# Sample states read before their update, the update in the MLP, and a new start and end in a one-layer decoder step

## The chip, the cores and the metric

The kernel runs on one core of one Trainium2 chip. The metric is the device time of one execution in microseconds (us), the median of three runs. Engines are named as the profile names them: PE multiplies matrices, PEld loads its weights, DVE and ACT do elementwise work, POOL and SP here mostly issue DMAs (POOL also does a little arithmetic). SPq, POOLq and ACTq are the DMA queues of SP, POOL and ACT.

## The reference, cut to what matters

One layer of a decoder step is computed for a prompt of 256 tokens and for 8 sample tokens, each of which brings its own recurrent states. D_MODEL is 2048, all data is float32.

```
mod = silu(c) @ w_ada + b_ada                 # 2048 x 12288; sh1, sc1, gt1, sh2, sc2, gt2
h   = rmsnorm(x) * g * (1 + sc1) + sh1
z   = h @ w_in                                # 2048 x 15376
# A: spatial gating; B: HGRN2 recurrence (8 heads, dk = dv = 128)
# C: gated linear attention (4 heads, dk 128, dv 256)
S_t = diag(f_t) S_{t-1} + k_t v_t^T ;  o_t = S_t^T q_t        # B and C, per head
merged = sum_n sigmoid(z_gate[n]) * (branch[n] @ w_branch[n])
x = x + gt1 * rmsnorm(merged @ w_out) * g_post
h2 = rmsnorm(x) * g * (1 + sc2) + sh2
y2 = square(relu(h2 @ w_mlp_up)) @ w_mlp_down                 # 2048 x 8192 and back
x = x + gt2 * rmsnorm(y2) * g_post2
outputs: y_prompt, y_sample, final states of the prompt,
         updated states of the 8 samples (8 x 8 x 128 x 128 and 8 x 4 x 128 x 256), v rows
```

A sample is one token long, so its recurrence is one step: S = diag(f) S0 + k v^T and o = S^T q. The same output is also o = S0^T (f q) + (q . k) v, which needs the old state only.

## The kernel before, in words

**Products.** Activations stand transposed, with 264 columns (256 prompt tokens, 8 samples). Each float32 product is three PE products: weights and activations are both split into a high part and a low part, and PE adds hi by x-hi, hi by x-lo and lo by x-hi (lines 601, 602, 603 of `granule`). Weights come in granules of 128 x 4 x 256 (0.5 MB, the size of a buffer `raw`): `Stream.load` issues their DMAs on SP, up to LOAD_AHEAD = 5 granules ahead into 4 buffers, `Stream.split` splits them up to SPLIT_AHEAD = 2 granules ahead into 6 buffers of halves. A half is split by one ACT copy (`whi`, L109) and one DVE subtraction (`wlo`, L106). One granule is 24 products on PE.

**Stages.** (1) The first phase, in which chunks of the modulation (w_ada) are computed while the first columns of w_in already run, chunk by chunk: `First` loads w_ada (L273 are its products), and `at` and `at_batches` set the granule at which a load, a batch of products or a pair of x tiles (`modulate`) stands. PE's accumulators (`mm`, two buffers) go back through an ACT or DVE copy, or through a DVE add (L103, at L819) from the second chunk on. (2) The mixers and the three branches; (3) w_out; (4) the first MLP granules; (5) the MLP, 8 blocks of `up` and `down`; (6) the end: the norm of the MLP's output, the residual sum and the writes.

**Background work.** Between granules, `background()` lets two queues of generators advance: `bg` (the prompt's mixers) and `bs` (the samples), each by a rate. A generator that yields a condition is held until it is true; `now` counts granules. `samples_r(G)` runs in `bs`, for two groups of HGRN heads and one of GLA. In 8 steps for an HGRN group (4 heads each) and 16 for GLA (2 heads each), 32 in all, it fetches a state of 256 KB by POOL (`st`, L1073, 4 buffers) and the value rows spread over all partitions (`vbc`, L1079, 2 buffers, from the DRAM scratch `vs_d`), scales the state on ACT (L1099), adds k v on DVE (L1101) and writes it by POOL (L1102). The updated state then stays until `slot()` multiplies it on PE with the masked queries `qm` (L640) and adds the rows to `os_`. FETCHED = 3 is the number of granules that a fetch is given to land. The 32 steps are 96 instructions on each of ACT and DVE.

**Order.** Instructions are placed on their engines by a scheduler, except where a manual_schedule holds an engine to the written order: all engines in the first phase (L112 to L838), PE and POOL in the mixers and branches (L963 to L1398), PE in w_out, PE, DVE, ACT and POOL in the first MLP granules (L1515 to L1769), and PE alone in the MLP and the end (L1770 to L1822). In the MLP, ACT, DVE and POOL are thus placed by the scheduler. `now` and the generators set the written order only.

**End.** The last down tile (two 128-row halves, `gated(7, ...)`, L1414) is added, squared into `sqacc`, gated and transposed; `norms()` (L1456) multiplies the squares by ones, the root follows (L194), and each piece of the output is either a DVE multiply-add or (the three `by_pe` pieces) two products on PE, one with the identity for x1 and one with the diagonal of the norm. L1812 issues the writes on SP and ACT.

## Time and profile before

| what | value |
|---|---|
| runs | 1937.14, 1937.15, 1942.04 us; median 1937.15 |
| profiled execution's own time, its span | 1936.48 us, 1934.7 us |
| busy: PE, PEld | 1900.5 us (98%), 1811.2 us (94%) |
| busy: DVE, ACT, POOL | 1191.7 us (62%), 996.9 us (52%), 87.7 us (5%) |
| DMA | 442.06 MB, 228 GB/s over the span |
| weights' queue (SP), POOL's queue | 409.62 MB, 28.48 MB |

How to read it: the span runs from the first to the last instruction; the run's own time has 1.8 us more around it. A row of a stretch has, after its bounds and its length, the busy time and count of PE, PEld, DVE, ACT and POOL, then the granted clock of PE, the busy share of the DMA engines and their GB/s. A row of the timeline has the start, the duration, the engine, the line and the operation; in brackets stands the idle time ahead of it and what ended it. A row of a group has count, busy time, mean ns of one, idle time ahead and its main releaser. In rows of DMA issues the last number is the median us from issue to landing.

### The profile page before, as it was taken

Reading aid. Unit: us, or ns where it says so; the run is one execution under the profiler, and the core shown is the slowest. Engines: PE = TensorE matmul, PEld = TensorE weight load, DVE = VectorE, ACT = ScalarE, POOL = GpSimd, SP = SyncE. Lnnn points to the kernel's source line nnn. Section 1 sums busy time; section 2 is a strip of 40 time slices with the busy share of each in tenths; the row PEclk is TensorE's granted clock in tenths of the full one; section 3 lists DMA queues with packets and bytes.
Section 4 is the critical chain, followed back from the end, with each engine's and each line's share of the span. In section 5 each row is a group of like instructions: output and inputs, shape, how many; then the busy total and the mean of one; then the engine's idle time right before and its main releaser. Section 6 shows DMA issues by size and latency. Waiting matters only on the chain.

```text
span 1934.7 us, 42322 instructions
## 1 busy us (share of the span) xinstructions
PE 1900.5 (98%) x17092; PEld 1811.2 (94%) x17092; DVE 1191.7 (62%) x2129; ACT 996.9 (52%) x1812; POOL 87.7 (5%) x144
## 2 busy tenths in 40 slices
...
GB/s 325 349 319 236 226 307 206 226 254 252 184 269 278 221 260 277 309 264 251 251 252 231 304 143 193 230 239 188 183 178 183 182 179 184 176 184 179 181 183 102
DMA packets 339380, 442.06 MB, mean 228 GB/s; under 512 B 14930, under 2 KB 281024, under 8 KB 339184
## 3 DMA queue, kind: packets, MB, share of 16 engines
q1 hardware_dynamic: 329120, 409.62, 65.6%
q0 software_dynamic: 8992, 28.48, 4.6%
...
## 4 chain that ended last, share of the span: by engine, by line
PE 94%; DVE 2%; DMA 2%; ACT 1%; issue 1%; POOL 0%; SPq 0%; DVEq 0%; ACTq 0%
PE mm L601 29%; PE mm L602 28%; PE mm L603 28%; PE ada L341 3%; PE ada L273 2%; DMA vbc<-vs_d 1%; PE sm L633 1%; DVE wlo L106 1%; PE sm L845 1%; PE sm L640 0%; DMA st<-in_state_gla_dram 0%; DMA b<-in_x_prompt_dram 0%; DVE b L103 0%; DMA b<-in_w_ada_dram 0%; ACT b L109 0%
## 5 line engine op out<-in xcount | busy, mean ns | idle before, releaser
L601 PE MATMUL mm<-b,whi 128*128 128x264 f32 x4592 | 1318.1, 287 | 5.7 <-DVE b L103 2.9
L602 PE MATMUL mm<-b,whi 128*128 128x264 f32 x4592 | 1307.7, 285 | 1.4 <-DVE b L106 1.2
L603 PE MATMUL mm<-b,wlo 128*128 128x264 f32 x4592 | 1305.1, 284 | 3.1 <-DVE wlo L106 2.6
L106 DVE TENSOR_TENSOR wlo<-raw,whi 128x512 fp32r<-128x512 f32 x1136 | 770.3, 689 | 498.0 <-ACT whi L109 495.4
L109 ACT CAST whi<-raw 128x512 fp32r<-128x512 f32 x1132 | 692.3, 618 | 726.9 <-PE mm L602 648.2
L601 PEld LDWEIGHTS mm<-b,whi 128*128 128x128 f32 x4592 | 865.4, 188 | 49.2 <-issue 24.7
L603 PEld LDWEIGHTS mm<-b,wlo 128*128 128x128 f32 x4592 | 865.5, 188 | 3.7 <-DVE wlo L106 3.7
L602 PEld LDWEIGHTS mm<-b,whi 128*128 128x128 f32 x4592 | 865.5, 188 | 2.4 <-DVE b L106 1.3
L103 DVE TENSOR_TENSOR b<-b,mm 128x528 f32<-128x528 f32 (+1 forms) x137 | 95.7, 700 | 98.2 <-PE mm L603 98.2
L1101 DVE SCALAR_TENSOR_TENSOR st<-vbc,b,st 128x128 f32<-128x128 f32 (+1 forms) x96 | 34.2, 391 | 54.7 <-DMA vbc<-vs_d 49.8
L1099 ACT ACTIVATE st<-st,fs 128x128 f32<-128x128 f32 (+1 forms) x96 | 37.0, 430 | 58.7 <-DMA st<-in_state_hgrn_dram 32.5
L273 PE MATMUL ada<-b,cT 128*32 128x256 f32 (+1 forms) x640 | 34.7, 354 | 6.9 <-DMA b<-in_w_ada_dram 6.8
L341 PE MATMUL ada<-araw,cT 128*32 128x512 f32 x296 | 39.9, 601 | 0.0
L273 PEld LDWEIGHTS ada<-b,cT 128*32 128x32 f32 x640 | 17.8, 112 | 18.8 <-ACT b L234 6.1
L100 DVE TENSOR_TENSOR b<-b,b 128x512 f32<-128x512 f32 (+1 forms) x47 | 34.1, 742 | 1.4 <-ACT b L1209 0.9
L1102 POOL DMA_DIRECT2D out_dram<-st x32 | 23.5, 735 | 156.4 <-DVE st L1101 155.6
L341 PE MATMUL ada<-b,cT 128*32 128x512 f32 x216 | 25.8, 593 | 0.0
L106 DVE TENSOR_TENSOR b<-gt,b 128x528 fp32r<-128x528 f32 x32 | 22.7, 708 | 3.6 <-ACT whi L109 0.5
L106 DVE TENSOR_TENSOR b<-b 128x1024 f32<-128x1024 f32 (+1 forms) x24 | 24.3, 1018 | 0.0
L100 DVE TENSOR_TENSOR gt<-vt 128x528 f32<-128x528 f32 x32 | 22.5, 702 | 0.9 <-ACT vt L1729 0.9
L1735 ACT ACTIVATE b<-vt 128x528 fp32r<-128x528 f32 x32 | 20.7, 647 | 1.0
L341 PEld LDWEIGHTS ada<-b,cT 128*32 128x32 f32 x216 | 6.9, 110 | 15.1 <-issue 14.6
...
## 6 DMA issues: line engine op xcount, KB each, us to landing
raw<-in_w_in_dram SPq DMA_DIRECT2D x232, 512.0 KB, 4.6
raw<-in_w_mlp_up_dram SPq DMA_DIRECT2D x128, 512.0 KB, 3.7
raw<-in_w_mlp_down_dram SPq DMA_DIRECT2D x128, 512.0 KB, 3.6
b<-in_w_ada_dram SPq DMA_DIRECT2D x102, 512.0 KB, 6.3
araw<-in_w_ada_dram SPq DMA_DIRECT2D x74, 512.0 KB, 5.4
raw<-in_w_branch_dram SPq DMA_DIRECT2D x48, 512.0 KB, 4.3
raw<-in_w_out_dram SPq DMA_DIRECT2D x32, 512.0 KB, 4.2
b<-in_w_ada_dram SPq DMA_DIRECT2D x32, 256.0 KB, 6.5
```

What stands on the lines that cost most here:

```text
L100: V.tensor_tensor(o, a, b, op=ALU.mult)
L103: V.tensor_tensor(o, a, b, op=ALU.add)
L106: V.tensor_tensor(o, a, b, op=ALU.subtract)
L109: S.copy(hi, src)
L273: T.matmul(acc[32 * j:32 * j + 32, 0:n], cT[:, k, :], w[:, n * j:n * j + n], start=k == 0, stop=k == KT - 1)
L341: T.matmul(self.acc[32 * j:32 * j + 32, :], cT[:, k, :], ws[j // 2][:, j % 2 * 512:j % 2 * 512 + 512], start=k == 0, stop=k == KT - 1)
L601: T.matmul(o, a, xh(k + j), start=first and j == 0, stop=False)
L602: T.matmul(o, a, xl(k + j), start=False, stop=False)
L603: T.matmul(o, b, xh(k + j), start=False, stop=last and j == n - 1)
L1099: S.activation(st[:, i, :], st[:, i, :], AF.Copy, scale=fs[:, h0 + i, b:b + 1])
L1101: V.scalar_tensor_tensor(st[:, i, :], v[:, i, :], k[:, h0 + i, NP + b:NP + b + 1], st[:, i, :], ALU.mult, ALU.add)
L1102: nc.gpsimd.dma_start(G.s_out(b, h0, nh), st)
```

## The change

**Start.** `cst` and `x_sample` are loaded by ACT's queue instead of SP's. The scaling of the last x tiles (`x_scaled`) moves out of the start to granules 1 and 2. For the first granule, `granule_by_part` runs the products by kind, and `modulate_first` makes both low parts of x before the low parts of the weights. The third chunk's loads, products and tiles stand one granule earlier (`at_batches(2, ...)`).

**Samples.** `samples_r` no longer updates a state. It makes `qf` = q f, masks that into `qm`, and starts `os_` with the value rows (transposed on PE) times q . k (a product with ones). States are fetched as before, every third into a `vbc` buffer, and go to `slot()` as loaded; FETCHED is 4. The factors f and k are kept in `kept`.

**Update.** A new generator `states()` fetches each state and its values again, scales, adds and writes them. It is appended to `bs` when the MLP starts, at a rate of 0.4.

**End.** The last two down tiles get an accumulator each; the products, sums, transposes and writes stand in a fixed order on PE, DVE and ACT; POOL makes the samples' output rows.

```diff
-FETCHED = 3
+FETCHED = 4
+UPDATE_RATE = 0.4
...
-    nc.sync.dma_start(cst[:, 0:256], consts[:, 0:256])
+    nc.scalar.dma_start(cst[:, 0:256], consts[:, 0:256])
...
-    nc.sync.dma_start(xsr, x_sample.rearrange("b o (k p) -> (b o k) p", p=P))
+    nc.scalar.dma_start(xsr, x_sample.rearrange("b o (k p) -> (b o k) p", p=P))
...
-    def x_scaled():
-        while late:
+    def x_scaled(n=2):
+        for _ in range(n):
...
-            more[j]()
+        for f in more:
+            f()
...
+    def granule_by_part(accs, xh, xl):
+
+        item, parts = stream[0].next()
+        _, k0, n, c0, width = item
+        for part, x, j in ((0, xh, 0), (0, xh, 1), (0, xl, 0), (0, xl, 1), (1, xh, 0), (1, xh, 1)):
+            for m in range(width // P):
+                T.matmul(accs[m // 2][:, m % 2, 0:NT], parts[j][part][:, 0, m * P:(m + 1) * P], x(j),
+                         start=part == 0 and x is xh and j == 0, stop=part == 1 and j == 1)
...
-            if sv[0][2] == 0:
-                V.tensor_copy(os_, po)
-            else:
-                add(os_, os_, po)
+            add(os_, os_, po)
...
-    x_scaled()
...
+    at(1, x_scaled, 1)
+    at(2, x_scaled, 1)
...
-    at_batches(2, (9, 11, 14, 17))
+    at_batches(2, (8, 10, 13, 16))
...
+            if gg:
+                granule(win, 0, n, begin[gi * gn][0], gn * CW, accs, hH, hL, k0, True, True, False)
+            else:
+                granule_by_part(accs, hH, hL)
...
+    kept = const([P, 3, 2, 4 * NS], "kept")
...
-        fs = tmp([P, 4, NS], "fs")
+        fs, ks = (kept[:, G.i, c].rearrange("p (h b) -> p h b", h=4) for c in range(2))
         S.activation(fs, g[:, :, NP:NT], AF.Exp)
-        qm = blk([P, 4, NS, 32])
-        mul(qm, q[:, :, NP:NT].unsqueeze(3).to_broadcast([P, 4, NS, 32]),
-            delta.rearrange("p (b c) -> p b c", b=NS).unsqueeze(1).to_broadcast([P, 4, NS, 32]))
+        V.tensor_copy(ks, k[:, :, NP:NT])
+        yield
         steps = [(b, h) for b in range(NS) for h in range(0, 4, nh)]
-        ahead, vals = [], []
+        ahead, fetched = [], [0]
 
         def fetch(b, h):
-            st = tmp([P, nh, dv], "st", ST_BUFS)
+            odd = fetched[0] % 3 == 2
+            fetched[0] += 1
+            st = tmp([P, nh, dv], "vbc" if odd else "st", VB_BUFS if odd else ST_BUFS)
             nc.gpsimd.dma_start(st, G.s_in(b, h, nh))
             ahead.append((st, now[0]))
 
-        def values(b, h):
-            v = tmp([P, 4, P], "vbc", VB_BUFS)
-            r0 = 4 * nj * b + h * nj
-            nc.gpsimd.dma_start(v, vs_d[G.i, r0:r0 + 4, :].partition_broadcast(P))
-            vals.append((v.rearrange("p (h j) v -> p h (j v)", h=nh), now[0]))
-
         for s in steps[0:2]:
             fetch(*s)
-            yield
-        values(*steps[0])
+        os_ = tmp([P, dv], f"os{G.i}", 1)
+        pads = tmp([P, 4, 32], "xsn", 1)
+        nc.gpsimd.memset(pads, 0.0)
+        for j in range(nj):
+            for i, b in enumerate(G.v):
+                V.tensor_copy(pads[:, i * nh:(i + 1) * nh, 0:NS], b[:, j::nj, NP:NT])
+            yield READY
+            yield READY
+            ps = sm([P, P])
+            T.transpose(ps, pads.rearrange("p h b -> p (h b)"), ident)
+            S.copy(os_[:, j * P:(j + 1) * P], ps)
+            yield
+        qf = tmp([P, 4, NS], "fs")
+        mul(pads[:, :, 0:NS], q[:, :, NP:NT], ks)
+        mul(qf, q[:, :, NP:NT], fs)
         yield
-        os_ = tmp([P, dv], f"os{G.i}", 1)
+        qm = blk([P, 4, NS, 32])
+        mul(qm, qf.unsqueeze(3).to_broadcast([P, 4, NS, 32]),
+            delta.rearrange("p (b c) -> p b c", b=NS).unsqueeze(1).to_broadcast([P, 4, NS, 32]))
+        yield READY
+        ps = sm([P, 8])
+        T.matmul(ps[:, 0:1], pads.rearrange("p h b -> p (h b)"), ones[:, 0:1], start=True, stop=True)
+        kq = tmp([P, 1], "sss", 1)
+        V.tensor_copy(kq, ps[:, 0:1])
+        yield
+        S.activation(os_, os_, AF.Copy, scale=kq)
+        yield
         sts = []
         for n, (b, h0) in enumerate(steps):
             if n + 2 < len(steps):
 
-                yield lambda: len(sts) + sum(len(x[3]) for x in samples) <= ST_BUFS - 3
+                yield lambda: len(sts) + sum(len(x[3]) for x in samples) <= ST_BUFS - 1
                 fetch(*steps[n + 2])
-            if n + 1 < len(steps):
-                values(*steps[n + 1])
-            yield lambda: now[0] >= max(ahead[0][1] + FETCHED, vals[0][1] + FETCHED - 1)
-            st, v = ahead.pop(0)[0], vals.pop(0)[0]
-            for i in range(nh):
-                S.activation(st[:, i, :], st[:, i, :], AF.Copy, scale=fs[:, h0 + i, b:b + 1])
-            for i in range(nh):
-                V.scalar_tensor_tensor(st[:, i, :], v[:, i, :], k[:, h0 + i, NP + b:NP + b + 1], st[:, i, :], ALU.mult, ALU.add)
-            nc.gpsimd.dma_start(G.s_out(b, h0, nh), st)
-            sts.append(st)
+            yield lambda: now[0] >= ahead[0][1] + FETCHED
+            sts.append(ahead.pop(0)[0])
...
+    def states():
+        todo = [(G, b, h) for G in Gs for b in range(NS) for h in range(0, 4, 512 // G.dv)]
+        ahead = []
+        def fetch(G, b, h):
+            nj, nh = G.dv // P, 512 // G.dv
+            st, v = tmp([P, nh, G.dv], "st", ST_BUFS), tmp([P, 4, P], "vbc", VB_BUFS)
+            nc.gpsimd.dma_start(st, G.s_in(b, h, nh))
+            r0 = 4 * nj * b + h * nj
+            nc.gpsimd.dma_start(v, vs_d[G.i, r0:r0 + 4, :].partition_broadcast(P))
+            ahead.append((st, v.rearrange("p (h j) v -> p h (j v)", h=nh), now[0]))
+        fetch(*todo[0])
+        yield
+        for n, (G, b, h) in enumerate(todo):
+            if n + 1 < len(todo):
+                fetch(*todo[n + 1])
+                yield 0.5
+            yield lambda: now[0] >= ahead[0][2] + FETCHED
+            st, v = ahead.pop(0)[0:2]
+            nh = 512 // G.dv
+            for i in range(nh):
+                f, k = (kept[:, G.i, c, (h + i) * NS + b:(h + i) * NS + b + 1] for c in range(2))
+                S.activation(st[:, i, :], st[:, i, :], AF.Copy, scale=f)
+                V.scalar_tensor_tensor(st[:, i, :], v[:, i, :], k, st[:, i, :], ALU.mult, ALU.add)
+                if i % 2:
+                    yield 0.5
+            nc.gpsimd.dma_start(G.s_out(b, h, nh), st)
+            yield
...
-        for m in range(8):
+        for m in range(8 if f < NFB - 1 else 7):
...
+    bs.g.append(states())
+    rate[:] = (0.0, UPDATE_RATE)
...
+    order = tc.manual_schedule(engines={mybir.EngineType.PE, mybir.EngineType.DVE, mybir.EngineType.Activation})
+    order.__enter__()
...
+    za, zb = new_acc(), new_acc()
+    zt = [za[:, 0, 0:NT], zb[:, 0, 0:NT]]
...
+    def gated_tile(i):
+        k = 14 + i
+        d = y2[3][:, 2 + i, :]
+        add(d, d, zt[i])
+        S.activation(sq[:, i, :], d, AF.Square)
+        V.tensor_scalar(g[:, i, 0:NP], d[:, 0:NP], G2[:, k, 0:1], None, ALU.mult)
+        mul(gs[:, k:k + 1, :], y2[3][:, 2 + i:3 + i, NP:NT], G2[:, k:k + 1, 1:NC])
...
+    last_products(0, 0)
+    last_products(0, 1)
+    gated_tile(0)
+    add(sqacc, sqacc, sq[:, 0, :])
+    while later:
+        later.pop(0)[1]()
+    last_products(1, 0)
+    pt = sm()
+    rows_tile(0)
+    last_products(1, 1)
+    first_part(0)
+    gated_tile(1)
+    ps = sm([P, 2 + NS])
+    for t in range(2):
+        for i, v in enumerate((sqacc, sq[:, 1, :])):
+            T.matmul(ps[:, t:t + 1], v[:, t * P:(t + 1) * P], ones[:, 0:1], start=i == 0, stop=i == 1)
+    for i, v in enumerate((sqacc, sq[:, 1, :])):
+        T.matmul(ps[:, 2:2 + NS], ones, v[:, NP:NT], start=i == 0, stop=i == 1)
+    r3 = tmp([P, 2 + NS], "nr", 1)
+    rstd_sqrt(ps, 1.0 / D, r3)
+    rows_tile(1)
+    first_part(1)
+    first_part(2)
...
+    Q.tensor_tensor(gs, gs, r3s.unsqueeze(1).to_broadcast([P, KT, NS]), op=ALU.mult)
+    Q.tensor_tensor(ys.rearrange("p b k -> p k b"), gs, xsT, op=ALU.add)
...
+    nc.sync.dma_start(y_sample.rearrange("b o (k p) -> (b o k) p", p=P), yo)
```

How the update moves in the built program is shown at three places. The first is DVE in branch 1's last tile (the product of the gate, `gt`, and its add to the sum, `b`); `wlo` is a half granule's low part, `st` a sample state, numbers tell buffers apart. Before:

```order
L106 TENSOR_TENSOR wlo_11183<-raw_11072,whi_11182 128x512
L106 TENSOR_TENSOR wlo_11221<-raw_11106,whi_11220 128x512
L106 TENSOR_TENSOR wlo_11225<-raw_11106,whi_11224 128x512
L103 TENSOR_TENSOR os_1521_9301<-os_1521_9301,sm_11230 128x256
L106 TENSOR_TENSOR wlo_11265<-raw_11147,whi_11264 128x512
L1342 SCALAR_TENSOR_TENSOR gt_11193<-gt_11193,mm_11195 128x528
L106 TENSOR_TENSOR wlo_11269<-raw_11147,whi_11268 128x512
L103 TENSOR_TENSOR b_7667<-b_7667,gt_11193 128x528
L106 TENSOR_TENSOR wlo_11304<-raw_11186,whi_11303 128x512
```

and now, at the same place (the sum is `b_7557`, the gate `gt_10976`):

```order
L1341 SCALAR_TENSOR_TENSOR st_17153<-vbc_17154,kept,st_17153 128x128 x4
L107 TENSOR_TENSOR wlo_10971<-raw_10854,whi_10970 128x512
L1341 SCALAR_TENSOR_TENSOR st_17426<-vbc_17427,kept,st_17426 128x128 x2
L107 TENSOR_TENSOR wlo_11004<-raw_10906,whi_11003 128x512
L1341 SCALAR_TENSOR_TENSOR st_17426<-vbc_17427,kept,st_17426 128x128 x2
L107 TENSOR_TENSOR wlo_11008<-raw_10906,whi_11007 128x512
L1341 SCALAR_TENSOR_TENSOR st_17654<-vbc_17655,kept,st_17654 128x128
L107 TENSOR_TENSOR wlo_11042<-raw_10940,whi_11041 128x512
L1341 SCALAR_TENSOR_TENSOR st_17654<-vbc_17655,kept,st_17654 128x128
L1396 SCALAR_TENSOR_TENSOR gt_10976<-gt_10976,mm_10978 128x528
L107 TENSOR_TENSOR wlo_11046<-raw_10940,whi_11045 128x512
L104 TENSOR_TENSOR b_7557<-b_7557,gt_10976 128x528
```

Before, one weight split follows another here, with the samples' sums (`os`) and the gate between; now state updates stand between the splits, four adds or two at a time. The rows of updates reach from DVE row 948 to 1100 of 2044, and from 707 to 822 of 1669 on ACT; 69 low parts of weights and the gates of branch 1's last three tiles and of branch 2's group stand among them on DVE.

The second place is POOL. Before, GLA's steps of `samples_r`:

```order
L1073 DMA st_10580<-in_state_gla_dram 128x2x256
L1079 DMA vbc_10582<-vs_d 128x512
L1102 DMA out_dram<-st_10292 128x2x256
L1073 DMA st_10813<-in_state_gla_dram 128x2x256
L1079 DMA vbc_10815<-vs_d 128x512
L1102 DMA out_dram<-st_10571 128x2x256
L1073 DMA st_10822<-in_state_gla_dram 128x2x256
L1079 DMA vbc_10824<-vs_d 128x512
L1102 DMA out_dram<-st_10580 128x2x256
```

and now, in the middle of `states()`:

```order
L1344 DMA out_dram<-st_16181 128x4x128
L1326 DMA vbc_16683<-vs_d 128x512
L1344 DMA out_dram<-st_16447 128x4x128
L1326 DMA vbc_16910<-vs_d 128x512
L1324 DMA st_17153<-in_state_hgrn_dram 128x4x128
L1324 DMA st_17426<-in_state_hgrn_dram 128x4x128
L1344 DMA out_dram<-st_16682 128x4x128
L1326 DMA vbc_17154<-vs_d 128x512
L1344 DMA out_dram<-st_16909 128x4x128
L1326 DMA vbc_17427<-vs_d 128x512
```

The written kernel puts the update behind the start of the MLP; on POOL its rows are 64 to 159, ahead of the loads of x1 (rows 160 to 163), which belong to w_out. Each fetch of values (`vbc`) stands behind the write of the state two before it.

The third is PE's first granule (`b_338` and `b_339` are x's high and low part). Before, its first half:

```order
L601 MATMUL mm_365<-b_338,whi_328 128x264
L602 MATMUL mm_365<-b_339,whi_328 128x264
L603 MATMUL mm_365<-b_338,wlo_329 128x264
L601 MATMUL mm_365<-b_338,whi_328 128x264
L602 MATMUL mm_365<-b_339,whi_328 128x264
L603 MATMUL mm_365<-b_338,wlo_329 128x264
L601 MATMUL mm_365<-b_338,whi_330 128x264
L602 MATMUL mm_365<-b_339,whi_330 128x264
L603 MATMUL mm_365<-b_338,wlo_331 128x264
L601 MATMUL mm_365<-b_338,whi_330 128x264
L602 MATMUL mm_365<-b_339,whi_330 128x264
L603 MATMUL mm_365<-b_338,wlo_331 128x264
```

and now, the whole granule:

```order
L615 MATMUL mm_363<-b_338,whi_328 128x264 x2
L615 MATMUL mm_364<-b_338,whi_328 128x264 x2
L615 MATMUL mm_363<-b_338,whi_330 128x264 x2
L615 MATMUL mm_364<-b_338,whi_330 128x264 x2
L615 MATMUL mm_363<-b_339,whi_328 128x264 x2
L615 MATMUL mm_364<-b_339,whi_328 128x264 x2
L615 MATMUL mm_363<-b_339,whi_330 128x264 x2
L615 MATMUL mm_364<-b_339,whi_330 128x264 x2
L615 MATMUL mm_363<-b_338,wlo_329 128x264 x2
L615 MATMUL mm_364<-b_338,wlo_329 128x264 x2
L615 MATMUL mm_363<-b_338,wlo_331 128x264 x2
L615 MATMUL mm_364<-b_338,wlo_331 128x264 x2
```

The low part of x is needed by the second product before, by the ninth to sixteenth now, and the low part of the weights by the last eight.

95 lines of the change are left out of this document (57 added, 38 removed).

## Prediction

> **What bounds the kernel now.** I read the page first, then the busy times in stretches of the span, and last the timeline around PE's longest waits.
>
> ```profile
> span 1934.7 us, 42322 instructions
> PE 1900.5 (98%) x17092; PEld 1811.2 (94%) x17092; DVE 1191.7 (62%) x2129; ACT 996.9 (52%) x1812; POOL 87.7 (5%) x144
> ...
> 0.00:20.00 20.00, 8.19 (x75) 3.83 (x75) 4.83 (x26) 6.55 (x12) 5.54 (x15) 1.00 0.87 286
> 40.00:110.00 70.00, 66.06 (x690) 60.45 (x689) 45.24 (x84) 29.80 (x52) 0.00 (x0) 1.00 0.93 331
> 400.00:500.00 100.00, 94.22 (x1176) 87.00 (x1175) 62.40 (x120) 52.77 (x110) 13.39 (x20) 0.97 0.78 246
> 1500.00:1600.00 100.00, 100.00 (x827) 100.00 (x826) 57.22 (x86) 46.98 (x77) 0.00 (x0) 1.00 0.60 182
> 1900.00:1935.00 35.00, 27.31 (x193) 23.70 (x191) 18.93 (x45) 13.20 (x28) 0.00 (x0) 0.97 0.23 77
> ```
>
> PE is busy for 1900.5 of 1934.7 us, so no more than 34 us can come from removing idle time. The rows are stretches, with the busy time and count of PE after each stretch's length. The idle time lies at the start (11.8 us), in 40 to 110 (3.9), in 400 to 500 (5.8) and at the end (7.7). In the MLP (1500 to 1600) there is none: 827 matmuls in 100 us are 0.121 us each, and a granule of weights, 24 matmuls, is 2.91 us. In 400 to 500 the granted clock is below 1 as well. Both waits there have one cause, the sample states:
>
> ```profile
> 443.71 0.75 POOL L1073 DMA_DIRECT2D st<-in_state_hgrn_dram  x1 [16.07 <-PE sm L640]
> 450.83 1.28 ACT L1099 ACTIVATE st<-st,fs 128x128 f32<-128x128 f32 x4 [4.34 <-DMA st<-in_state_hgrn_dram]
> 456.81 0.39 PE L603 MATMUL mm<-b,wlo 128*128 128x264 f32 x1 [1.91 <-DVE wlo L106]
> 460.29 0.42 PE L603 MATMUL mm<-b,wlo 128*128 128x264 f32 x1
> 460.95 0.42 PE L603 MATMUL mm<-b,wlo 128*128 128x264 f32 x1
> ...
> 476.35 0.63 ACT L1207 ACTIVATE b<-b 128x512 f32<-128x512 f32 x1 [2.58 <-DVE st L1101]
> 477.75 1.24 PE L1220 MATMUL sm<-b,b 128*128 128x128 f32 x8 [3.84 <-DVE b L100]
> 479.89 0.42 PE L603 MATMUL mm<-b,wlo 128*128 128x264 f32 x1
> 480.55 0.42 PE L603 MATMUL mm<-b,wlo 128*128 128x264 f32 x1
> ```
>
> POOL fetches a state late; ACT stands 4.34 us before it, with the weights' high parts queued behind; PE runs out of split weights and waits 1.91 us. Then it runs at half pace: three matmuls take 0.66 us instead of 0.364, from 458.1 to 461.6, which loses about 1.6 us. The second time ACT (L1207) waits for DVE's state update, PE waits 3.84 us and loses about 1.3 us more by the same slow pace (479.2 to 482). Together 1.9 + 1.6 + 3.8 + 1.3 = 8.6 us.
>
> **The change, part by part.**
>
> *Start.* The constants and x_sample leave SP's queue, so the x loads, and the w_ada loads behind them, are issued 0.9 us earlier (1.64 to 0.74, where SP's first issue stood).
>
> ```profile
> 0.74 0.38 SPq L117 DMA_DIRECT2D cst<-in_consts_dram  x1
> 1.64 1.88 SPq L136 DMA_DIRECT2D b<-in_x_prompt_dram  x4
> 12.40 3.32 PE L273 MATMUL ada<-b,cT 128*32 128x128 f32 x40 [6.00 <-DMA b<-in_w_ada_dram]
> 27.90 0.39 PE L601 MATMUL mm<-b,whi 128*128 128x264 f32 x1 [0.34 <-ACT b L429]
> 35.01 0.39 PE L601 MATMUL mm<-b,whi 128*128 128x264 f32 x1 [0.53 <-DVE b L819]
> ```
>
> PE waits 6.00 us for w_ada at 12.40, so the 0.9 us passes through to 27.90 if the DMAs are full from the first issue, and is nothing if they are not; I take 0.8. The small loads now queue on ACT, about 0.8 us later, under the 6 us for which PE waits anyway. In the first granule the eight products of high part by high part come first, and DVE makes x's low part ahead of the weights'. PE gains about 1.3 us there, but the next granule needs both accumulators back, and the second comes back by a DVE copy behind four weight splits (the wait of 0.53 at 35.01). That copy moves only by the x scaling that has left (one 0.64 us product), so I take 0.6 (0 to 1.3).
>
> *Second transition.* The w_ada pieces of the third chunk come a granule earlier. The waits at 104.64 and 107.70 are these:
>
> ```profile
> 104.64 0.36 PE L601 MATMUL mm<-b,whi 128*128 128x264 f32 x1 [2.22 <-DVE b L103]
> 107.70 0.39 PE L601 MATMUL mm<-b,whi 128*128 128x264 f32 x1 [1.36 <-ACT b L109]
> ```
>
> The first is an accumulator that waits behind DVE's making of the x tiles, and that order is kept, a granule earlier. The second, for the tiles, goes (1.36), but the adds of the last granule now stand behind the second pair of tiles, for a like time. Zero, between 4 gained and 1 lost.
>
> *Samples from the old state.* From 400 to 835 us ACT and DVE no longer scale and add states, and no vbc loads are fetched; PE reads the state as loaded, at least six granules after its fetch. So nothing on ACT or DVE stands before a state load, and the 8.6 us go (bounds: 0 and 9.5). New on PE are four transposes and three column products of 0.3 us and less, about 1 us lost.
>
> *The state update.* It is written into the MLP, where DVE and ACT have room. But ACT, DVE and POOL are not held to the written order there, and in the built program (the rows are shown with the change) all 96 pairs of ACT scale and DVE add stand among 69 weight splits (34.5 granules) from branch 1's sixth step to branch 2's first. Before the change that stretch runs from 802 to 912 us:
>
> ```profile
> 802.00:912.00 110.00, 109.79 (x914) 102.94 (x907) 63.97 (x117) 51.02 (x90) 9.99 (x15) 1.00 0.82 271
> 802.00:912.00 110.00, 4.48 (x10) 1.00 0.82 271
> q1 hardware_dynamic: 20239, 25.69, 71.2%
> q0 software_dynamic: 1200, 3.93, 10.8%
> raw<-in_w_in_dram SPq DMA_DIRECT2D x28, 512.0 KB, 4.6
> vbc<-vs_d POOLq DMA_DIRECT2D x5, 256.0 KB, 6.6
> L1101 DVE SCALAR_TENSOR_TENSOR st<-vbc,b,st 128x128 f32<-128x128 f32 (+1 forms) x96 | 34.2, 391 | 54.7 <-DMA vbc<-vs_d 49.8
> L1099 ACT ACTIVATE st<-st,fs 128x128 f32<-128x128 f32 (+1 forms) x96 | 37.0, 430 | 58.7 <-DMA st<-in_state_hgrn_dram 32.5
> ```
>
> The first row is the whole stretch (after PE and PEld stand DVE's and ACT's busy time, the clock, the DMA share and GB/s), the second DVE's state adds alone. Engines: DVE's 64.0 us less the 4.5 us of updates that stood there, plus 34.2, is 94 of 110. ACT has 51 less 3.7 plus 37, 84. Neither is the bound, but DVE has no time left to catch up after a wait.
>
> Bytes: 25.8 MB of weights, without 3.9 MB of state traffic, and 32 updates of three 262144-byte transfers, 25.2 MB: 51 MB. The busiest stretches reach
>
> ```profile
> 808.00:814.00 6.00, 6.00 (x52) 6.00 (x51) 3.46 (x7) 4.17 (x9) 0.71 (x1) 1.00 1.04 395
> 804.00:810.00 6.00, 6.00 (x53) 6.00 (x50) 0.12 (x2) 0.86 (x3) 1.91 (x3) 1.00 1.02 368
> ```
>
> 395 and 368 GB/s. 51 MB take 129 us at the one and 139 at the other, 19 to 29 us over 110; weights that already wait in the four buffers of 0.5 MB at the start give back up to 5. So at least 15 us are lost. A rule of the Trainium skill speaks here (DMA: Bandwidth & Descriptors, Specifications): it limits a core's HBM traffic to about 358 GB/s. By that rule bytes alone would take 142 us; the 395 GB/s of the row are over it, for 6 us.
>
> Latency: vbc has two buffers, and POOL fetches update n's values only after it has issued the write of update n-2, which waits for DVE. Now:
>
> ```profile
> 803.35 0.57 POOL L1079 DMA_DIRECT2D vbc<-vs_d  x1
> 809.94 0.88 DVE L1101 SCALAR_TENSOR_TENSOR st<-vbc,b,st 128x256 f32<-128x256 f32 x2 [5.88 <-DMA vbc<-vs_d]
> ```
>
> From issue to use 6.6 us pass, as in the median above, and DVE stands still for 5.88 us of them. PE loses nothing at that place, since the splits lead it by two granules, 5.8 us, and DVE then has 20 us to catch up. When updates follow each other that cover is spent after the first. A pair of updates costs 0.8 (hand-over and write issued) + 6.6 + DVE's adds with the split between them (2.0 for four heads, 1.0 for two): 9.4 and 8.4, mean 8.9 us. Fifteen pairs are 133 us, and the first two updates about 8.5: 142 us, 32 over 110. I take this, since bytes alone nearly ask for it too. Above it, if landing grows to 9 us with full DMAs: 15 x 11.3 + 11 = 180, 70 lost.
>
> *End.* The last two tiles get accumulators of their own.
>
> ```profile
> 1920.20 0.28 PE L603 MATMUL mm<-b,wlo 128*128 128x264 f32 x1
> 1923.64 0.27 ACT L194 ACTIVATE nr<-sm,eps 128x10 f32<-128x10 f32 x1 [0.65 <-PE sm L1461]
> 1929.90 1.07 ACTq L1812 DMA_DIRECT2D out_dram<-b  x2
> ```
>
> Now the norm's square root starts 3.2 us after the last product (to 1923.64), behind both tiles' squares. Afterwards only one add (0.4), one square (0.4), and six small products (1.3) lie between, with their hand-overs about 2.5 us: 0.7 gained. Behind it the identity products of x are out of the way, and the last write is issued about 1929.15 instead of 1930.97. I take 1.8 (0.5 to 3.5).
>
> Sum, against the profiled execution's own 1936.48: - 0.8 - 0.6 - 8.6 + 1.0 + 32 - 1.8 = +21.2, so 1957.7. The median of the runs, 1937.15, lies 0.7 above that execution; 1958 for the median.
>
> **Rivals.**
>
> *The updates are hidden, faster.* Mechanism: the two vbc buffers at the stretch above. It decides at 110 us for 16 pairs, 6.9 a pair, which is a landing of 4.6 us or less, and then the stretch costs nothing: 1937 - 10.8, 1926. For it: the other 0.5 MB loads of this stretch land in 4.6 us. Against it: the 51 MB do not fit at any rate shown. That the updates run in the MLP, as written, ends at the same time; only the built order speaks against it. Chance 0.11.
>
> *Bytes alone.* If landing stays short although the DMAs are full, 15 to 24 us are lost: 1941 to 1950. Chance 0.22.
>
> *Clock.* The half pace of 458 us came after a wait of 1.91 us. If waits in the stretch of 1 to 2 us an update hold PE there, 34.5 granules at 24 x 0.22 = 5.3 us take 182 us, 72 lost: 1998. For it: the rows at 460.29. Against it: 104.64, where 2.22 us were followed by no slow rows. Chance 0.07. The Trainium skill (TensorE: Matmul & The Clock Gate, HAM oscillation) asks only for no idle gaps over about 3.4 us. By that rule, waits of 1 to 2 us would leave the pace alone, and this rival would fall; the row at 456.81 does not agree with it.
>
> **How the numbers follow.** My forecast, latency and bytes together, 1950 to 1980, has 0.55; the rest, 0.05, is a loss that the gains just cancel, within 6 us of before. About 0.3%, 6 us, is what a measurement can tell from no change (the runs of before spread from 1937.14 to 1942.04). Faster 0.11, same 0.05, slower 0.84. The range runs from 1938 (the byte bound, with first granule and end at their upper bounds) to 1990 (landing grown to 8.5 us), and leaves out the hidden case and the clock.
>
> **What would show it.** Right: the updates' ACT and DVE rows lie between about 790 and 940 us; DVE's waits for vbc there sum to tens of us; PE's busy time in that stretch falls to some three quarters, on weight-split waits; DMA share near 1.0; no wait of PE or ACT at 450 to 480; PE flat in the MLP; last write about 2 us nearer to the last product. Wrong: updates rows after 1180 us, or a PE without idle time from 800 to 950. If slow rows fill that stretch, it is the clock.

## The result

The changed kernel takes 1994.71 us (median of 4 runs, 1993.35 to 1995.82), the kernel before 1937.14 beside it: a ratio of 1.0299, 95% interval 1.0286 to 1.0312. It is slower by 57 us, where 21 had been forecast (1958, range 1938 to 1990). The sign and the place were right, the size was not. The profiled execution took 1993.35 us.

The page of the changed kernel, its span and the engines:

```profile
span 1991.2 us, 42429 instructions
PE 1926.5 (97%) x17108; PEld 1832.7 (92%) x17108; DVE 1198.7 (60%) x2141; ACT 1001.8 (50%) x1819; POOL 112.5 (6%) x181
```

PE is busy for 26 us more than before, though it makes nearly the same products, and idle for 30.5 us more: 64.7 of 1991.2 us, before 34.2. Both parts lie in one place. The busy times in stretches (after the length PE, PEld, DVE, ACT, POOL; then granted clock, DMA share, GB/s):

```profile
750.00:800.00 50.00, 50.00 (x402) 44.23 (x400) 21.22 (x43) 26.22 (x58) 8.52 (x12) 1.00 0.78 254
800.00:850.00 50.00, 41.34 (x283) 37.83 (x281) 23.45 (x62) 23.81 (x62) 16.31 (x24) 0.84 0.82 257
850.00:900.00 50.00, 40.12 (x249) 37.27 (x250) 25.66 (x61) 23.27 (x58) 20.26 (x30) 0.85 0.92 284
900.00:950.00 50.00, 33.05 (x233) 28.74 (x232) 21.98 (x45) 17.84 (x38) 21.26 (x32) 0.86 0.90 307
950.00:1000.00 50.00, 45.89 (x359) 42.22 (x358) 32.68 (x55) 24.72 (x43) 5.45 (x8) 0.97 0.89 302
```

From 800 to 975 us PE falls to 41, 40 and 33 of 50 us, and its granted clock to 0.84 to 0.86. The waits there, by the engine that waits (total, times, longest):

```profile
PE mm L603 <- ACT whi L110: 20.0, 9, 10.3
PE mm L605 <- DVE wlo L107: 17.9, 16, 2.9
```

```profile
DVE st L1341 <- DMA vbc<-vs_d: 28.4, 12, 4.5
DVE st L1341 <- ACT st L1340: 15.5, 2, 8.3
DVE st L1341 <- DMA out_dram<-st: 11.7, 4, 5.2
```

```profile
POOL st L1324 <- DMA out_dram<-st: 56.3, 23, 6.1
POOL out_dram L1344 <- DVE st L1341: 43.3, 17, 11.6
```

PE waits for both parts of the weights, DVE for the values and for the scaled states, and POOL for the landing of state writes. The adds themselves:

```profile
L1341 DVE SCALAR_TENSOR_TENSOR st<-vbc,kept,st x96: 342/349/486, 803.3 to 975.1; 128x128 f32<-128x128 f32 x64, 128x256 f32<-128x256 f32 x32
```

They run from 803.3 to 975.1: 172 us for 32 updates, 10.7 a pair.

The same 1136 low parts of weights are made by DVE in the same order in every kernel here, so the difference in the start of the n-th of them (counted from 0) tells where time is lost. This table is worked out from the traces (us, difference to before; E1 to E8 are told below):

| split | before, at | after | E1 no update | E2 written order | E3 bunched in MLP | E4 start back | E8 |
|---|---|---|---|---|---|---|---|
| 4 | 33.05 | +1.34 | +0.98 | +1.24 | +1.20 | -0.54 | |
| 60 | 154.96 | +0.59 | +0.60 | +0.52 | +0.46 | -1.27 | -0.89 |
| 160 | 333.06 | +0.61 | +0.63 | +0.54 | +0.46 | -1.27 | |
| 400 | 779.33 | -8.19 | -7.57 | -7.59 | -8.41 | -10.15 | -9.34 |
| 500 | 943.80 | +55.75 | -8.78 | -8.85 | -9.62 | -11.36 | -10.61 |
| 640 | 1176.09 | +55.39 | -7.38 | -9.20 | -9.98 | -11.69 | -10.93 |
| 720 | 1300.07 | +55.64 | -7.14 | -8.98 | +50.28 | -11.46 | |
| 1100 | 1858.07 | +57.07 | -5.71 | -7.55 | +51.71 | -10.03 | -9.27 |
| end of span | 1934.7 | +56.5 | -6.3 | -8.4 | +51.1 | -10.6 | -10.1 |

Read down the column "after": the start costs 1.3, the second transition gives 0.7 back, the samples give 8.8, the updates cost 63.9 between splits 400 and 500, 1.3 goes in the MLP, and the end gives 0.6: together 56.5.

### The profile page after: what moved, and what is told of

It reads as the page before. It is cut to its first block, busy times and chain, and to the rows that moved or that the text cites. A ratio compares the mean times of both kernels' runs of the same rounds, so it can differ in the third digit from the quotient of the medians.

```text
span 1991.2 us, 42429 instructions
## 1 busy us (share of the span) xinstructions
PE 1926.5 (97%) x17108; PEld 1832.7 (92%) x17108; DVE 1198.7 (60%) x2141; ACT 1001.8 (50%) x1819; POOL 112.5 (6%) x181
## 4 chain that ended last, share of the span: by engine, by line
PE 80%; issue 9%; DMA 6%; DVE 2%; POOL 1%; ACT 1%; SPq 0%; ACTq 0%; DVEq 0%; POOLq 0%
PE mm L603 24%; PE mm L604 24%; PE mm L605 24%; DMA out_dram<-st 2%; PE ada L342 2%; PE ada L274 1%; DMA st<-in_state_hgrn_dram 1%; DVE wlo L107 1%; DMA st<-in_state_gla_dram 1%; POOL st L1324 1%; DMA vbc<-vs_d 1%; DMA b<-in_w_ada_dram 1%; PE sm L644 1%; PE sm L857 1%; DMA b<-in_x_sample_dram 0%
## 5 line engine op out<-in xcount | busy, mean ns | idle before, releaser
L1340 ACT ACTIVATE st<-st,kept 128x128 f32<-128x128 f32 (+1 forms) x96 | 36.2, 428 | 92.7 <-DMA st<-in_state_gla_dram 28.4
L1341 DVE SCALAR_TENSOR_TENSOR st<-vbc,kept,st 128x128 f32<-128x128 f32 (+1 forms) x96 | 33.8, 392 | 63.1 <-DMA vbc<-vs_d 28.4
L274 PEld LDWEIGHTS ada<-b,cT 128*32 128x32 f32 x640 | 17.9, 114 | 14.0 <-DMA b<-in_w_ada_dram 5.0
```

Source lines behind the costliest of these rows:

```text
L274: T.matmul(acc[32 * j:32 * j + 32, 0:n], cT[:, k, :], w[:, n * j:n * j + n], start=k == 0, stop=k == KT - 1)
L1340: S.activation(st[:, i, :], st[:, i, :], AF.Copy, scale=f)
L1341: V.scalar_tensor_tensor(st[:, i, :], v[:, i, :], k, st[:, i, :], ALU.mult, ALU.add)
```

## The experiments

### Is it the update, and is it the place?

Three kernels: the change without the update (E1), the update held where it is written (E2), and the update bunched as closely but in the MLP (E3). The edits are shown shortened.

```diff
 E1: -    bs.g.append(states())
 E2: -    order = tc.manual_schedule(engines={PE})                      # around the MLP
     +    order = tc.manual_schedule(engines={PE, DVE, Activation, Pool})
 E3:      bs.g.append(states())
     +    V.scalar_tensor_tensor(kept, first MLP block, 0.0, kept, ALU.mult, ALU.add)
```

> The changed kernel without its state update: the updated sample states are not computed and not written (two outputs are left out), everything else stands as changed. Theory A (the 57 us come from the updates standing among branch 1's weight splits, and nothing else of the change costs more than 3 us): in the changed kernel's trace the weight splits stand 8.2 us earlier than before the change at 780 us and 55.7 us later at 960 us, so 64 us go, 1928 to 1932 us. Rival B (the clock or the new PE work of the samples costs a part of it): 1940 us or more. PE has no half pace and no wait over 1 us between 700 and 1000 us by A.

> The changed kernel with DVE, ACT and POOL held to the written order in the MLP, so that the updates stand where they are written, some 14 weight splits to an update. Theory A (the place is the cause, and in the MLP, with DVE 58% busy and 180 GB/s, an update's landing passes while splits are ahead): as without the update, 1928 to 1934 us. Rival B (each update's wait for its loads stops DVE and with it PE wherever it stands): 32 updates of 2 us or more, 1990 us or more. Rival C (the written order of ACT and DVE itself costs, by accumulators that come back later): 1935 to 1960 us with waits of PE spread evenly over the MLP.

> The changed kernel with the update's factors made to depend on the first MLP block, so that the scheduler places all updates, as closely as in the changed kernel (32 updates among some 60 weight splits), at the start of the MLP instead of branch 1. Weights ask for 180 GB/s there and not 250. If bytes set the loss: 30 granules of 0.5 MB and 25 MB of updates are 41 MB, 108 us at 380 GB/s over 87 us, no more than 20 us lost, 1950 us. If the round of an update (fetch, scale, add, write, landing, 10.75 us a pair as measured) sets it: 172 us over some 90 to 100, 70 to 80 us lost, 2000 us. If landing is quicker there (3.6 instead of 4.5 us for weights): 8 us a pair, 130 us, 1965 us.

E1 took 1930.58 us (ratio to before 0.9970, 0.9959 to 0.9981), E2 1928.46 (0.9962, 0.9949 to 0.9975), E3 1987.59 (one run). In E1, the stretch has no idle time and full clock:

```profile
800.00:900.00 100.00, 100.00 (x831) 95.49 (x831) 56.71 (x98) 46.27 (x78) 0.00 (x0) 1.00 0.75 232
900.00:1000.00 100.00, 100.00 (x827) 94.45 (x826) 53.34 (x77) 44.12 (x71) 0.00 (x0) 1.00 0.79 254
```

The spans of the two lie 62.8 us apart, the medians 64.1. So the update costs all that the changed kernel loses, and theory A holds. E2 makes the same updates with the same transfers, and loses nothing by them; its stretch of the updates, and DVE's state adds with what ended the idle time before them:

```profile
1216.00:1730.00 514.00, 514.00 (x4215) 508.27 (x4214) 315.07 (x520) 273.88 (x496) 61.30 (x91) 1.00 0.77 237
```

```profile
L1341 DVE SCALAR_TENSOR_TENSOR st<-vbc,kept,st x96: 343/347/480, 1215.8 to 1730.1; 128x128 f32<-128x128 f32 x64, 128x256 f32<-128x256 f32 x32
its engine sat idle before it (us, times) until:
who waited for it (us, times):
```

Under the line on idle time stands nothing: with 16 us between updates every load has landed before DVE comes to it, and PE is busy for 514 of 514 us. E3 has the updates bunched at 1178 to 1328 us, where the weights ask for 180 GB/s only:

```profile
1178.00:1328.00 150.00, 109.83 (x741) 99.63 (x734) 73.12 (x163) 69.31 (x160) 59.76 (x89) 0.87 0.88 285
L1341 DVE SCALAR_TENSOR_TENSOR st<-vbc,kept,st x96: 342/347/486, 1178.1 to 1327.7; 128x128 f32<-128x128 f32 x64, 128x256 f32<-128x256 f32 x32
```

```profile
PE mm L605 <- DVE wlo L107: 22.3, 17, 6.9
PE mm L603 <- ACT whi L110: 10.5, 4, 4.0
```

The updates take 150 us, beside 54 splits, which are 27 granules of work, and 60 us are lost between splits 640 and 720. It is not branch 1, nor its denser weights, but the bunching: the byte forecast of 20 us fails, and the forecast by rounds (70 to 80 lost, or 1965 with quicker landing) has the measured time between its two figures, with 9.4 us a pair.

### What holds a bunched update?

The transfers were taken away in turn, at the place where the changed kernel has them. These kernels add a constant in place of the values (E5), leave the states unwritten (E6), or both (E7).

```diff
 E5: -            nc.gpsimd.dma_start(v, vs_d[...].partition_broadcast(P))    # and v = att[:, 0:4, :]
 E6: -            nc.gpsimd.dma_start(G.s_out(b, h, nh), st)
 E7: both
```

> The changed kernel without the loads of the value rows in the update (8.4 MB; a constant tile is added instead, so the sample states come out wrong). The scheduler then sets the 32 updates among 46 weight splits, 23 granules, 67 us of PE. Measured is the time from the first to the last state add (172 us in the changed kernel, 10.75 a pair) and the loss over the kernel without an update (63 us). Theory P (the prediction's: the two value buffers set the round): nothing of the round is left, under 80 us for the updates, 10 us lost, 1940. Theory W (the landing of a state's write sets it: POOL issues the next state fetch ahead of the next write, and waits there until the write before has landed): the round loses two issues of 0.57 only, 9.6 a pair, 150 us, 75 to 85 us lost, 2010. Theory M (bytes): 34 MB at the 283 GB/s of the stretch, 120 us, 45 us lost, 1976.

> The changed kernel without the writes of the updated states (8.4 MB, two outputs are left out), the same bytes less as without the value loads. The scheduler sets the 32 updates among 50 weight splits, 25 granules, 73 us. Theory W: the waits for landing writes go, and the round falls to that of the value buffers, 0.57 and 6.1 landing and about 1.5 on DVE, 8.2 a pair, 127 us, 45 us lost, 1976. Theory P (values set the round, writes cost an issue of 0.74 only): about 10 a pair, 155 us, 75 lost, 2005. Theory M (bytes): as without the value loads, 120 us.

> The changed kernel with neither value loads nor writes in the update: 32 state fetches into four buffers, scale and add are left (41 splits, 20 granules, 60 us). Theories W and P: no DMA waits for another, so a fetch lands 5.7 us after its buffer is free with four under way, about 2 us an update: 60 to 80 us, at most 20 lost, 1931 to 1950. Theory B (the half pace of PE, or ACT and DVE work among the splits, is a loss of its own): 30 us lost or more, 1960, with the granted clock at half for 20 us or more of the stretch.

They took 1976.08, 1984.24 and 1944.10 us (one run each). The state adds of each:

```profile
L1340 DVE SCALAR_TENSOR_TENSOR st<-att,kept,st x96: 337/348/487, 800.4 to 922.4; 128x128 f32<-128x128 f32 x64, 128x256 f32<-128x256 f32 x32
```

```profile
L1341 DVE SCALAR_TENSOR_TENSOR st<-vbc,kept,st x96: 342/349/485, 802.9 to 936.2; 128x128 f32<-128x128 f32 x64, 128x256 f32<-128x256 f32 x32
```

```profile
L1340 DVE SCALAR_TENSOR_TENSOR st<-att,kept,st x96: 338/347/486, 800.7 to 879.9; 128x128 f32<-128x128 f32 x64, 128x256 f32<-128x256 f32 x32
```

Without values the updates take 122 us (7.6 a pair), without writes 133 (8.3), with neither 79 (5.0). Theory P asked for under 80 in E5 and 155 in E6: it falls. Theory W asked for 150 and 127: right for E6, wrong for E5. Theory M asked for 120 in both: near in both. No single transfer holds the round; each of the two takes about as much out. E7 loses 14 us against E1, with half pace for 3.4 us only, where theory B asked for 30 or more: it falls. How much of the 14 us is ACT's and DVE's work among the splits, and how much the fetches that are left, these runs do not part.

Then POOL's order, the weights' bytes, PE's pace and the number of value buffers.

```diff
 E11: -    order = tc.manual_schedule(engines={PE})                       # around the MLP
      +    order = tc.manual_schedule(engines={PE, Pool})
 E9:  +            nc.sync.dma_start(t[:, 0, :], w[k * P:(k + 1) * P, c0:c0 + width])       # branches 1 and 2
      +            self.raw[i] = [t[:, 0:1, :].to_broadcast([P, 2, width])] * 2
 E10: -                    T.matmul(o, a, xl(k + j), start=False, stop=False)               # branches 1 and 2
 E12: -VB_BUFS = 2
      +VB_BUFS = 4
      -SPLIT_BUFS = 6
      +SPLIT_BUFS = 5
```

> The changed kernel with only POOL held to the written order in the MLP's part of the program. The updates stay where they are (70 weight splits among them, before 69), with the same transfers and buffers, but POOL now issues fetch and values of the next update and then one write, so a state fetch waits for a write issued two updates earlier and not for the one just issued. Theory W (POOL stands on the landing of a write, 5.2 us, with the next write and the next values behind it): the round falls from 10.7 to what the value buffers alone ask for, 8.3 to 9 a pair as without the writes; updates 133 to 144 us, 25 to 36 us lost against the kernel without an update, 1956 to 1967. Theory M (the DMA engines' time, 149 us): 155 to 165 us, 45 to 55 lost, 1976 to 1986. If neither: as the changed kernel, 1994.

> The changed kernel with only a quarter of each weight granule loaded in branches 1 and 2 (the first of four k blocks, read four times by the splits; the outputs come out wrong). Orders, waits and the work of PE, DVE and ACT stay: 32 updates among 68 splits. In the changed kernel the DMA engines are 0.88 busy for the 169 us of the updates at 281 GB/s, so 149 us of DMA time, of which the 18 MB of these weights are some 55. Theory M (the DMA engines' time, 320 GB/s when full, sets the stretch): 149 less 42 is 107 us, no more than the stretch takes unhindered (110), so at least 40 of the 64 us go: updates in 115 to 130 us, 1935 to 1955. Theory W (a chain of landings, each 5 to 6 us, one behind the other on POOL): landings get a little shorter, 9.5 to 10.5 a pair, 150 to 168 us, 40 to 58 lost, 1970 to 1988.

> The changed kernel without the products of the weights' high part by the activations' low part in branches 1 and 2 (a third of PE's products there; the outputs lose accuracy), so that PE asks for weights faster; the scheduler then sets the 32 updates among 108 splits, 54 granules, 105 us of PE. Measured is the time from the first to the last state add (172 us as changed). Theory M (DMA time): 28 MB of weights in place of 18, 20 to 25 us more: 190 to 200 us. Theory W (landings behind each other): 165 to 178 us as before. Theory C (PE's half pace is what holds the stretch, since the weights' splits wait for PE): a third fewer products for each granule but half as many granules again, 172 us too, but then PE stands on the chain of waits for most of it; by M and W it stands there for less than a tenth.

> The changed kernel with four value buffers in place of two; the room for them is taken from the split weights (5 buffers of halves in place of 6, so PE's lead is half a granule shorter and a loss of its own may come from that all along the kernel). The scheduler sets the 32 updates among 51 weight splits, 25 granules, 74 us of PE. What tells is the time from the first to the last state add (172 us as changed, 174 with POOL in written order). Theory P (two value buffers, one landing of 6 to 7 us a pair, hold the round): values no longer hold it, and what is left is the ring of four states, fetch, scale and add, write and landing, some 14 us for four: 100 to 120 us. Theory M (the DMA engines' time): 25 MB of updates, 13 of weights and some 5 of w_ada at 320 GB/s, never more than 0.93 busy: 145 us or more. Theory W (POOL's wait for landing writes): 155 to 172 us.

Stretches from the first to the last state add, by the profile's windows, with the splits counted in the traces (E9, E10 and E12 are one run each):

| run | weight splits among the updates | updates, us | a pair | granted clock | DMA share, GB/s | us in all |
|---|---|---|---|---|---|---|
| after | 68 | 172 | 10.7 | 0.86 | 0.88, 283 | 1994.71 |
| E3 in the MLP | 54 | 150 | 9.4 | 0.87 | 0.88, 285 | 1987.59 |
| E5 no values | 46 | 122 | 7.6 | 0.90 | 0.83, 276 | 1976.08 |
| E6 no writes | 50 | 133 | 8.3 | 0.90 | 0.83, 259 | 1984.24 |
| E7 fetch only | 41 | 79 | 5.0 | 0.98 | 0.85, 275 | 1944.10 |
| E9 quarter weights | 68 | 156 | 9.8 | 0.90 | 0.75, 230 | 1978.69 |
| E10 fewer products | 108 | 207 | 12.9 | 0.85 | 0.92, 311 | 1931.05 |
| E11 POOL as written | 70 | 174 | 10.9 | 0.88 | 0.88, 286 | 1993.75 |
| E12 four value buffers | 51 | 136 | 8.5 | 0.90 | 0.92, 305 | 2017.94 |

E11 (ratio to before 1.0299, 1.0282 to 1.0316) decides against theory W as it was put. POOL's wait for landing writes is gone, and nothing is won. Theory M's 155 to 165 us for the updates are missed as well: they take 174. The chain of waits from 810 to 920 us, summed by line, of the changed kernel and of E11:

```profile
by line: issue 39.4%; DMA out_dram<-st 34.3%; DMA st<-in_state_hgrn_dram 11.9%; POOL st L1324 9.9%; POOL vbc L1326 2.5%; POOL out_dram L1344 2.0%; DVE st L1341 2.0%; ACT whi L110 1.7%; DVE wlo L107 0.7%; ACT st L1340 0.4%; POOLq L1344 0.1%;
```

```profile
by line: DMA vbc<-vs_d 47.6%; DMA st<-in_state_hgrn_dram 16.1%; issue 13.7%; DVE st L1341 7.9%; POOL out_dram L1344 6.7%; ACT st L1340 3.2%; POOL st L1324 2.9%; DVE wlo L107 2.9%; ACT whi L110 1.9%; DVEq L1341 0.3%; DVE sa L185 0.2%; ACTq L
```

In the changed kernel the landing of writes stands for 34.3% and that of values is not among the lines; in E11 values stand for 47.6% and the landing of writes is not among them, and the updates take as long. The largest share of the changed kernel, "issue", lies mostly on POOL between two state fetches, where POOL's own waits name the writes' landing too (the 56.3 us above). In both kernels no PE row is among these lines, and over all of the updates PE's rows are 1.2% of the chain in the changed kernel and none in E11 (worked out from the traces). That speaks for PE's half pace falling into time in which it would have waited otherwise. The rounds of E11 can be read off POOL:

```profile
851.40 0.76 POOL L1344 DMA_DIRECT2D out_dram<-st  x1 [6.63 <-DVE st L1341]
852.15 0.75 POOL L1324 DMA_DIRECT2D st<-in_state_hgrn_dram  x1
852.88 0.55 POOL L1326 DMA_DIRECT2D vbc<-vs_d  x1
860.89 0.76 POOL L1344 DMA_DIRECT2D out_dram<-st  x1 [5.10 <-DVE st L1341]
870.70 0.76 POOL L1344 DMA_DIRECT2D out_dram<-st  x1 [5.16 <-DVE st L1341]
882.25 0.76 POOL L1344 DMA_DIRECT2D out_dram<-st  x1 [6.02 <-DVE st L1341]
```

The first add on the values that were issued at 852.88:

```profile
858.86 0.35 DVE L1341 SCALAR_TENSOR_TENSOR st<-vbc,kept,st 128x128 f32<-128x128 f32 x1 [2.96 <-DMA vbc<-vs_d]
```

A pair from 851.40 to 860.89 is 9.5 us: a write issued (0.76), a state fetch issued (0.75), then the values, issued at 852.88; the first add is at 858.86, and with adds and splits the next write can go at 860.89. It is the round that had been forecast, 9.4, with the state fetch's issue added (0.75) and the values in use 0.6 us sooner than the 6.6 taken; the next pairs take 9.8 and 11.6.

E9 leaves orders and work alone and takes 13 MB of weights off the DMA engines (48.7 MB among the updates become 35.6): 172 goes to 156 us, and 1978.69 is in theory W's range and outside of theory M's (1935 to 1955). With the DMA engines 0.75 busy, bytes alone do not hold its 156 us. E10 puts more on them, and the updates take 207 us, nearer to M's 190 to 200 than to W's 165 to 178; PE's rows are 6.8% of its chain of waits over the updates, less than the tenth that M and W asked for, against theory C. The time that it saves on PE is in its 1931 us and says nothing here. E12 has 136 us, between P (100 to 120) and M (145 or more), with DMA engines 0.92 busy; against E1, its 2017.94 us hold 25 us that are lost before the updates and 10 behind them, with fewer split buffers all along the kernel, and 55 in the stretch.

The landings behind these times, in the profile's DMA rows between 803 and 975 us (count, KB each, median us from issue to landing), of the changed kernel, of E9 and of E10:

```profile
vbc<-vs_d POOLq DMA_DIRECT2D x31, 256.0 KB, 6.1
out_dram<-st POOLq DMA_DIRECT2D x31, 256.0 KB, 5.2
```

```profile
vbc<-vs_d POOLq DMA_DIRECT2D x31, 256.0 KB, 5.3
out_dram<-st POOLq DMA_DIRECT2D x32, 256.0 KB, 4.7
```

```profile
vbc<-vs_d POOLq DMA_DIRECT2D x26, 256.0 KB, 6.7
out_dram<-st POOLq DMA_DIRECT2D x26, 256.0 KB, 5.9
```

With the DMA engines 0.75, 0.88 and 0.92 busy, values take 5.3, 6.1 and 6.7 us to land and writes 4.7, 5.2 and 5.9, and a pair of updates takes 9.8, 10.7 and 12.9 us. Among these three kernels, which move the same transfers through the same buffers, landings grow with the load of the DMA engines. Beyond them the values do not follow the share: they take 6.3 us in E2 at 0.77, 6.6 before at 0.82, and 6.8 in E11 at 0.88. What follows: a bunched update is held by landings that stand one behind the other on a few buffers, and cutting the chain at one place moves it to the next, as from writes to values in E11. How much of the 172 us the load alone would ask for stays open: 48.7 MB (283 GB/s for 172 us) take 151 us at a full share (283 / 0.88 = 322 GB/s), and the same chain with 13 MB less takes 156. The two bounds lie too close together for these runs to part them.

The runs also show why easing the update wins so little. The builder's order puts 41 to 70 splits (108 in E10, with fewer products for each), 60 to 105 us of PE's work at full clock, beside the updates, and the updates take 1.3 to 2.0 times as long in every run; where the update is eased, it is packed closer (E12: 51 splits where 68 stood). That the scheduler sets them by shorter transfers than these is an inference from the counts.

### The start and the end

```diff
 E4 (on E2): -    nc.scalar.dma_start(cst[:, 0:256], consts[:, 0:256])
             +    nc.sync.dma_start(cst[:, 0:256], consts[:, 0:256])
             (and x_sample alike)
 E8 (on E4): y_sample's copy before put((1, 0, 0)), its write before put((1, 1, 512))
```

> The kernel with the MLP in written order, and besides the constants and x_sample loaded on SP's queue again, as before the change. Theory A (the small loads, queued on ACT behind 2 MB of x, land 3 us later and push PE's first products to 5.97 us; the first w_in product then starts at 30.18 instead of 27.90): the first w_in product at 27.5 to 28.5 us, and 2 us less than with the start as changed. Rival B (w_ada's landing sets the start anyway): no difference beyond 0.5 us.

> MLP in written order, constants and x_sample on SP's queue, and at the end y_sample's write ahead of the last prompt write instead of behind all. Theory: in the changed kernel the last write, of y_sample, is issued at 1986.37 and the span ends 4.4 us later; ahead of the last prompt write it costs ACT nothing (it stands idle from 1984.65 to 1985.09), and the last issue ends 0.7 us earlier: the span from the last product to the end 12.6 to 13.0 us instead of 13.4, 1925 to 1928 us in all. Rival: the end is set by the landing of the 256 KB prompt writes, no difference.

PE's first waits, in the changed kernel:

```profile
5.97 0.26 PE L151 MATMUL sm<-cst,b 16*128 16x16 f32 x1 [5.97 <-DMA b<-in_c_prompt_dram]
8.57 0.47 PE L152 MATMUL sm<-cst,b 128*128 128x128 f32 x1 [2.34 <-DMA b<-in_c_sample_dram]
10.03 0.48 PE L219 MATMUL sm<-cst,b 128*128 128x128 f32 x1 [0.99 <-DMA b<-in_x_sample_dram]
12.11 0.59 PE L211 MATMUL sm<-sqs,cst 128*128 128x8 f32 x2 [1.61 <-DVE sqs L104]
12.91 1.19 PE L274 MATMUL ada<-b,cT 128*32 128x128 f32 x16 [0.20 <-ACT b L235]
30.18 0.75 PE L615 MATMUL mm<-b,whi 128*128 128x264 f32 x4 [0.34 <-ACT b L430]
```

and in E4:

```profile
5.80 0.59 PE L211 MATMUL sm<-sqs,cst 128*128 128x8 f32 x2 [1.60 <-DVE sqs L104]
12.27 2.52 PE L274 MATMUL ada<-b,cT 128*32 128x128 f32 x32 [5.88 <-DMA b<-in_w_ada_dram]
28.31 0.75 PE L615 MATMUL mm<-b,whi 128*128 128x264 f32 x4 [0.34 <-ACT b L430]
```

The small loads land 3 to 7 us later, behind x, and three products wait for one of them each: the norm's products (L211) move from 5.80 to 12.11. The larger effect is on SP, and theory A does not have it. In the traces the landings of x_sample and of the first w_ada load are told by the same semaphore, and SP issues the second load only when the first has landed (before at 3.57 after 3.31, now at 10.00 after 9.99). In the changed kernel that is a wait of 7.2 us, and at its end the DMA engines stand still from 10 to 11 us:

```profile
SPq L454 <- DMA b<-in_x_sample_dram: 7.2, 1, 7.2
10.00:11.00 1.00, 0.48 (x1) 0.18 (x1) 0.42 (x2) 0.99 (x4) 0.00 (x0) 1.00 0.00 0
```

In E4 the first w_ada load is issued at 3.68. Since x lands sooner in the changed kernel (its last part at 9.82, in E4 at 11.64), the first w_ada product moves by 0.6 only (12.27 to 12.91), but the eighth w_ada load lands at 18.99 instead of 17.52, and the products in order behind it start 1.5 us later. That is most of the 1.9 us by which the first w_in product moves; the other 0.4 were not followed. E4 took 1928.33 us (0.9959, 0.9945 to 0.9974), no different from E2 in its runs; in the traces it is 1.8 us ahead at every split from number 4 to 160, and 2.2 at the end of the span. Theory A's times are met and rival B's are not, though the landing of w_ada is part of the path.

The end of the changed kernel:

```profile
1977.52 0.29 PE L1858 MATMUL mm<-b,wlo 128*128 128x264 f32 x1
1980.11 0.27 ACT L195 ACTIVATE nr<-sm,eps 128x10 f32<-128x10 f32 x1 [1.37 <-PE sm L1897]
1985.70 0.34 ACTq L1922 DMA_DIRECT2D out_dram<-b  x1
1986.37 0.45 SPq L1939 DMA_DIRECT2D out_dram<-xsn  x1
```

From the end of the last product (1977.81) to the last issue's end (1986.82) it is 9.0 us, before 10.5 (1920.48 to 1930.97); to the span's end 13.4, before 14.2. E8's runs (1927.29 us, ratio 0.9953, 0.9940 to 0.9967, 5 runs) are not clear of E4's, and its end in the trace is 13.1: 0.3 won, of the 0.4 to 0.8 expected. E8 has the lowest median of all kernels here with all outputs, 0.5% below the kernel before.

## Why the prediction was right or wrong

*State update: place and sign right, size wrong by half.* Forecast were +32, measured +63.9. The step that failed is the term "A pair of updates costs 0.8 + 6.6 + DVE's adds ... 8.9 us": measured were 10.7 a pair, 172 us instead of 142, and the 30 us between are the error. The landing of values was not the error (6.6 taken, 6.1 measured). What the sum left out stands on POOL's queue within the round: the issue of a state fetch (0.75), and, in the order as built, that fetch's wait for the landing of the write just issued (56.3 us in 23 waits). That wait is not the whole of it, since E11 lost as much without it: there, values landed later (6.8), and a pair still took 10.9. E6 supports this from the other side: where no state is written, a pair takes 8.3 us, which is about what the sum priced, though with 8 MB less on the DMA engines. The second error is one of form. The bounds from bytes and from landings were worked out beside each other and the larger was taken, while in E9, the changed kernel and E10 the second grows with the first. Of the signs named, two held (DVE waits 28 us for values, PE is busy for 132 of the 172 us, 77%); the DMA share is 0.88 and not near 1.0, and the updates reach to 975 us and not 940.

*Bytes: the rate was read from the wrong rows.* 368 and 395 GB/s stood over 6 us each. The row of the whole stretch, quoted in the prediction, says 271 GB/s at a share of 0.82, which is 330 at full (an estimate); 51 MB at that are 155 us, and the bound from bytes alone would have been 45 lost instead of 19 to 29. With it, 1958 could not have been the middle. The Trainium skill's limit (DMA: Bandwidth & Descriptors, Specifications), about 358 GB/s, gave an estimate of 142 us and was nearer to the 172 than the 129 of the row with 395; of the changed kernel's 40 slices of 50 us none passes it:

```profile
GB/s 315 348 323 216 236 306 220 213 233 203 239 233 186 251 221 241 264 285 294 306 281 245 269 212 142 235 229 212 180 181 180 180 181 181 180 180 180 180 181 107
```

*The upper end.* "If landing grows to 9 us: 70 lost" is what nearly came (64), by another sum: the landing of values did not grow, but more landings stood behind each other. The range ended at a landing of 8.5 us, 1990, short of this case.

*The clock, as a rival, came near by chance.* Its price was 1998, and PE's clock did fall to half for 48 of the 172 us. In PE's own time that is 24 us of the 64, and waits are the other 40; the condition of the rival, half pace through the stretch, was met only in part. PE's rows are next to nothing on the chain of waits (1.2%), and E10, with a third fewer products, spends longer there. Both speak for the half pace as a consequence of the waits and not their cause, but no run here keeps the clock up among the updates, so this is argued and not shown.

*Hidden updates.* Rejected rightly for the order as built. Where the order is the written one (E2), they are hidden, and the time, 1928.46, is near the 1926 of that case.

*Samples from the old state.* Forecast -8.6 and +1.0, measured -8.8 in all between splits 160 and 400, and in E1 another -1.2 up to split 500. No wait of PE over 1 us and no half pace is left from 400 to 500, as said.

*Start.* Forecast -0.8 and -0.6; measured +1.3. The failed step is that the w_ada loads behind x "are issued 0.9 us earlier". The first x load was (0.74 instead of 1.64), but the first w_ada load was issued 6.4 us later, behind x_sample's landing at 9.99. Before, the same wait stood there and cost little, with x_sample landed at 3.31. That the small loads wait "under the 6 us for which PE waits anyway" failed with it. The first granule gave more than its 0.6: from its first product to split 4 it is 0.9 us shorter, in the changed kernel and in E4, within the 0 to 1.3 of the forecast.

*Second transition.* Forecast 0, measured -0.7.

*End.* Forecast -1.8 on the last issue, measured -1.5 there, but the span ends only 0.6 to 0.8 earlier: y_sample's write goes last, and 4.4 us pass from the end of its issue to the span's end, where it was 3.7 before.

*Not foreseen:* 1.3 us between splits 500 and 1100, also in E2 (1.3) and E1 (3.1, with one half pace at 1137 us). Its cause stays open.
